# Six PSUM banks for the late tiles of an output projection, a feed-forward that starts in other banks, and a root on ScalarE

## The chip, the cores and the metric

The kernel runs on one core of a Trainium2 chip. The core has TensorE for matmuls (PE in the profile, its weight loads PEld), VectorE (DVE), ScalarE (ACT), GpSimd (POOL), a queue of DMA issues on SyncE (SP), SBUF as working memory and PSUM, eight banks of 128 partitions x 512 float32, for the results of matmuls. The metric is the device time of one execution in microseconds (us), median of several.

## The reference

One layer of a hybrid trunk in float32: 2048 tokens with 16 meta tokens ahead of them, model width 1024. What matters here:

```python
mixed = concat([lru_group, forgetting_attention, rwkv7_group]) @ w_out      # 1024 x 1024
h = h + rms_norm(mixed, norm_mix_post)
f = causal_dwconv(rms_norm(h, norm_ffn_pre) @ ffn_up, ffn_conv)             # 1024 -> 2 x 2816
gate, val = split(f)
f = (gelu(gate) * val) @ ffn_down                                           # 2816 -> 1024
h = h + rms_norm(f, norm_ffn_post)

def rms_norm(x, g):
    return x * rsqrt(mean(x * x, axis=-1) + 1e-6) * g
```

Each norm needs one reciprocal root for each token: a column of 128 values for a tile of 128 tokens.

## The kernel before, in words

The program is a line of stages: input projection beside the recurrences, attention, output projection, up projection of the feed-forward, down projection. Every matrix product is done with operands split in a high and a low part: three matmuls (L150, L151, L152) for each product of 128 rows. The up and down projections use seven products of half-size operands for eight (Strassen's scheme), whose operands are sums made on POOL and split by ACT (high, L1528) and DVE or POOL (low, L1529).

**The output projection** (`w_out_tile`, L1421) goes over 17 tiles of tokens, one of two tokens and sixteen of 128, numbered 0 to 16. For a tile it loads the mixed heads (raw, L143), splits them into `mh` (ACT, L144) and `ml` (DVE, L145), two buffers each, and computes two halves of 512 columns. A half takes 24 matmuls into one PSUM bank. Then `add_normed` (L1444) squares both halves on ACT with the sums in two columns (L1450), adds these (DVE, L1451), finds the reciprocal root with a seed from the bits and three Newton steps on 128 x 1 columns (DVE, L84 to L89, in `rstd_from`), scales the halves in their banks (L1456) and adds them to the residual (L1457), which is the last reader of the bank. The result is stored (L1440), and a second sum of squares (ACT, L96) and a second root (L84 to L89 on `rsv`) prepare the norm of the feed-forward. `mh` also takes the unused outputs of the squares.

`Banks` (L1399) hands out the banks of the halves. Up to tile 7 they come from two banks in turn (`ps_wo`); then `wide` is set, and a third bank joins (`ps_wo2`, the one that `ps_more` had during attention). Tiles 0 to 6 are mixed into attention, and tiles 7 and 8 (`HELD`) are held until attention's last step but one, so that they fill PE in its last step.

**PSUM.** In attention five banks are one pool (`ps_at`: two for maxima and sums, two for scores, one for values), `ps_more` has one and `ps_wo` two. After attention `ps_n` (two banks, for the transposes of `ffn_norm`) and `ps_f0` (three banks) take the place of the five. After the output projection `ps_f1` takes the three banks of `ps_wo` and `ps_wo2`. One unit of the up projection (342 tokens of two blocks by 128 columns of gate and value) uses three banks x, y, z; the units alternate between `ps_f0` and `ps_f1`. With `turn = 0` ahead of the loop (L1654) the first unit has `ps_f1`.

**Beside the late tiles**, from tile 8 on, the feed-forward is prepared: `ffn_norm` (L1484) loads finished tiles again, scales them (L1490) and transposes them (L1495) into the operands' quarters, POOL makes the sums of the first weights (L1601) and of the quarters (L1523), and as many operands as have memory are split: `uw0` (four weights) and `xo0` to `xo2` (three token operands). The other weights (`uw1`) and `xo3` to `xo7` lie in memory that the output projection's pool `wp` holds to its end.

**Order.** The program text gives each instruction a priority, and a planner puts the instructions of each engine in an order by simulating them; at run time each engine goes through its own list strictly in order and waits on semaphores. Pools marked `early` wait only for the tiles that lay in the same memory.

Lines that the change touches: `rstd_of` (L93), `Banks` (L1399 to L1408), `add_normed` (L1451, L1452), `turn` in `ffn_up` (L1654), the construction of `Banks` (L1996) and the line that sets `wide` (L2007). `add_normed` is also called by `Down.second` in the down projection, sixteen times.

Of the kernel before, what the change touches and what calls it, by code (L numbers as in the profile page):

```python
# [8 lines left out]
F32 = mybir.dt.float32  # L9
# [3 lines left out]
AF = mybir.ActivationFunctionType  # L13
ALU = mybir.AluOpType
# [4 lines left out]
P = 128  # L19
D = 1024  # L20
# [4 lines left out]
EPS = 1e-6  # L25
# [7 lines left out]
class Core:  # L33


    def __init__(self, tc, ctx):
        self.tc = tc
        self.nc = tc.nc
        self.ctx = ctx
        self.uid = 0  # L40
        nc = self.nc
        self.const = ctx.enter_context(tc.tile_pool(name="const", bufs=1))
        self.ident = self.const.tile([P, P], F32, name="ident")
        make_identity(nc, self.ident[:])
        self.flip = 0

    def n(self, s):
        self.uid += 1
# [41 lines left out]
    return y  # L90


def rstd_of(core, v, src, width, junk):  # L93

    ss = v[:, 4:5]
    core.nc.scalar.activation(junk, src, AF.Square, accum_out=ss)  # L96
    return rstd_from(core.nc, v, ss, width)

# [1300 lines left out]
class Banks:  # L1399


    def __init__(self, core, pools):
        self.core, self.pools, self.wide, self.turn = core, pools, False, 0

    def next(self):
        self.turn = (self.turn + 1) % 3 if self.wide else 0
        third = self.turn == 2
        return self.pools[third].tile([P, 512], F32, tag="wo", name=self.core.n("pswo"), bufs=1 if third else 2)  # L1408


def w_out_load(core, pool, w_out):
# [32 lines left out]
def add_normed(core, pool, halves, rows, gain, x, junk):  # L1444

    nc = core.nc
    v = pool.tile([P, 8], F32, tag="rs2", name=core.n("rs2"))
    s0, s1 = v[:rows, 4:5], v[:rows, 5:6]
    for c, acc in ((0, s0), (1, s1)):
        nc.scalar.activation(junk[c][:rows], halves[c][:rows], AF.Square, accum_out=acc)  # L1450
    nc.vector.tensor_tensor(s0, s0, s1, op=ALU.add)  # L1451
    r1 = rstd_from(nc, v[:rows], s0, D)  # L1452
    for c in range(2):
        cs = slice(512 * c, 512 * c + 512)
        y = halves[c][:rows]
        nc.vector.scalar_tensor_tensor(y, y, r1, gain[:rows, cs], op0=ALU.mult, op1=ALU.mult)  # L1456
        nc.vector.tensor_tensor(x[:rows, cs], x[:rows, cs], y, op=ALU.add)  # L1457
# [165 lines left out]
def ffn_up(core, raws, ring, pool, banks, w_up, cw, scr, between, tokens):  # L1623

    nc = core.nc
    tt, stt = nc.vector.tensor_tensor, nc.vector.scalar_tensor_tensor
    turn = 0
    units = [(sup, j) for sup in range(SUPERS) for j in range(NFF)]  # L1630
    ahead = UpWeights(core, raws, ring, w_up, scr, 0, 0)
    ws = [ahead.operand(i) for i in range(7)]
    xs = [tokens(0, i) for i in range(7)]

    def conv(src, u, j, n):
        y = pool.tile([P, FBLK], F32, tag="uy", name=core.n("uy"), bufs=UY)
        cc = u * NFF + j
        nc.scalar.activation(y[:, :n], src[:, 2 : n + 2], AF.Copy, scale=cw[:, 88 + cc : 89 + cc])  # L1638
        for i in (1, 0):
            stt(y[:, :n], src[:, i : n + i], cw[:, 44 * i + cc : 44 * i + cc + 1], y[:, :n], op0=ALU.mult, op1=ALU.add)  # L1640
        if u == 0:
            nc.scalar.activation(y[:, :n], y[:, :n], AF.Gelu_apprx_tanh)
        return y

    def ending(g, v, j, b0, n):
        core.pooled = nc.gpsimd.tensor_tensor(v[:, :n], g[:, :n], v[:, :n], op=ALU.mult)  # L1646
        nc.sync.dma_start(scr["ff"][P * j : P * j + P, b0 : b0 + n], v[:, :n])

    for at, (sup, j) in enumerate(units):
        b0 = [FBLK * (2 * sup + i) for i in range(2)]  # L1650
        n = [min(FBLK, SEQ - b) for b in b0]
        s = lambda tag: pool.tile([P, FN], F32, tag=tag, name=core.n(tag), bufs=1 if tag == "u2" else 2)[:]
        between(sup, j)
        more = at + 1 < len(units)  # L1654
        if more:
            ahead = UpWeights(core, raws, ring, w_up, scr, *units[at + 1][::-1])
        ws_next, bank = [], {}
        turn ^= 1
        for i, (name, (_, _, at_)) in enumerate(PRODUCTS.items()):
            w, x = ws[i], xs[i]  # L1660
            first = at_ not in bank
            if first:
                bank[at_] = banks[turn].tile([P, 512], F32, tag="up", name=core.n("psu"))[:, :FN]
            ps = bank[at_]
            for k in range(HK):
                mm3(nc, ps, w[:, 0, k], w[:, 1, k], x[:, 0, k], x[:, 1, k], first and k == 0, k == HK - 1, not first)
            if j == NFF - 1 and more:
                xs[i] = tokens(sup + 1, i)
            if more:
                ws_next.append(ahead.operand(i))  # L1670
            if name == "p1":
                ga = s("ga")
                nc.scalar.activation(ga, ps, AF.Copy)
            elif name == "p5":
                vb = s("vb")
                nc.scalar.activation(vb, ps, AF.Copy)
            elif name == "p6":
                u2 = s("u2")
                nc.scalar.activation(u2, ps, AF.Copy)
            elif name == "p3":  # L1680
                tt(ps, ps, u2, op=ALU.add)
                gb = conv(ps, 0, j, n[1])
            elif name == "p7":
                tt(vb, ps, vb, op=ALU.add)  # L1684
                vb = conv(vb, 1, j, n[1])
            elif name == "p2":
                tt(ps, ps, ga, op=ALU.add)
                ga = conv(ps, 0, j, n[0])
                ending(gb, vb, j, b0[1], n[1])
            else:  # L1690
                va = conv(ps, 1, j, n[0])
                ending(ga, va, j, b0[0], n[0])
        ws = ws_next
# [137 lines left out]
LATE = 8  # L1831
# [59 lines left out]
def hybrid_block_kernel(ctx: ExitStack, tc: tile.TileContext, args, out):  # L1891
    a = {s: v[0] if s != "meta_tokens" else v for s, v in args.items()}
    nc = tc.nc
    core = Core(tc, ctx)
# [86 lines left out]
    with ExitStack() as p3:  # L1981
# [11 lines left out]
        rs = {}  # L1993
        with p2:
            ps_wo.append(pool(p2, "ps_wo2", 1, space=PSUM, **right))
            banks = Banks(core, ps_wo)  # L1996
            g_post = spread(pool(p2, "gpost", 1, **right), a["norm_mix_post"], "g_post")
            wp = pool(p2, "wp", 2, **right)
            w = w_out_load(core, wp, a["w_out"])
# [2 lines left out]
            for i, (f, rows) in enumerate(FFN_TILES):  # L2002
                with tc.issue_after(at.steps[-2].ins) if i in HELD else nullcontext():
                    _, rs[i] = w_out_tile(
                        core, wp, banks, scr, w, x, meta, g_post, f + META - HALO, rows, rsv[:, 6 * i : 6 * i + 6]
                    )
                banks.wide = i >= LATE - 1  # L2007
                if i >= LATE and todo:
                    q, f, rows = todo.pop(0)
                    ffn_norm(core, np_, ps_n, scr, f, rows, rs[q], g_fpre, quarters[0], 0)  # L2010
                    if not todo:
                        run(ffn_sums(core, quarters[0]))
# [106 lines left out]
```

## Time and profile before

| what | value |
|---|---|
| median of three runs | 3123.35 us (3115.73 to 3134.21) |
| profiled execution | 3122.89 us |
| its span, first to last instruction | 3121.2 us |
| mean granted clock of TensorE | 0.962 |
| PE busy | 2925.9 us (94%) |
| DVE, ACT, POOL busy | 2251.1, 1452.4, 1301.9 us |
| output projection's last tiles beside the preparation | about 1632 to 1715 us |
| first matmul of the up projection | 1720.22 us |

In the profile a row of groups reads: line, engine, operation, output <- input tiles, shapes, count, busy time. A row of a timeline reads: start, duration, engine, line, operation, tiles, count, and in brackets the idle time of the engine ahead of it and what ended that. A row of waits reads: engine, tile and line that waited, engine, tile and line that it waited for, total, times, longest. A row of stretches reads: from:to, length, then busy time and count of PE, PEld, DVE, ACT and POOL (the engines with nothing to show are left out when one tile is asked for), granted clock, share and rate of the DMA engines. `psu` are banks of the up projection, `pswo` of the output projection, `psd` of the down projection, `pst` transposes, `sc`, `po` and `mx` the scores, values and maxima of attention.

### The profile page before, as it was taken

What the parts mean: (1) busy time and instruction counts of PE and PEld (TensorE: products, weight loads), DVE (VectorE), ACT (ScalarE), POOL (GpSimd) and SP (SyncE); (2) the same over time, 40 slices, a digit from 0 to 9 for tenths busy, and PEclk for the clock granted to TensorE, in tenths of its full rate; (3) what the DMA queues carried; (4) which work ended last, traced back from release to release, by engine and by line L of the source; (5) the groups of instructions that cost most, each with busy time, mean ns of one, the idle gap of its engine ahead of it and who ended that gap; (6) DMA issues with size and microseconds to landing.
All of it is one profiled execution on the core that took longest, in us unless ns stands there. A gap on an engine that the chain in (4) does not pass through costs nothing. (4 is left out here: it accounts for less than half of the span.)

```text
span 3121.2 us, 52484 instructions
## 1 busy us (share of the span) xinstructions
PE 2925.9 (94%) x18488; PEld 2492.2 (80%) x18488; DVE 2251.1 (72%) x4585; ACT 1452.4 (47%) x2716; POOL 1301.9 (42%) x1436
## 2 busy tenths in 40 slices
PE   6988999999978999999998899999999999999998
PEld 6987998999855664665576899899999999787776
DVE  6247655676688778877758898888778787547777
ACT  4135334344544444445533555566666665324332
POOL 3310001101134365446733568743533334547665
PEclk9999999999988788999999899999999999999999
DMA  6664333353353235544236555565665565535454
GB/s 205 226 204 137 101 97 100 107 140 104 97 143 81 64 84 142 130 117 107 65 107 201 162 171 158 167 193 170 166 166 166 166 188 162 174 105 167 143 161 142
DMA packets 456503, 443.72 MB, mean 142 GB/s; under 512 B 82496, under 2 KB 373514, under 8 KB 453408
## 3 DMA queue, kind: packets, MB, share of 16 engines
q1 hardware_dynamic: 455856, 439.99, 48.3%
q8 instruction: 145, 2.38, 0.3%
q14 instruction: 118, 0.97, 0.1%
q0 software_dynamic: 384, 0.39, 0.0%
HBM read 314.39 MB, written 125.87 MB: 141 GB/s over the span
## 5 line engine op out<-in xcount | busy, mean ns | idle before, releaser
L150 PE MATMUL psu<-xo,uw 128*128 128x344 f32 x1848 | 594.9, 326 | 25.2 <-DVE vb L1684 10.4
L151 PE MATMUL psu<-xo,uw 128*128 128x344 f32 x1848 | 597.1, 323 | 0.7 <-DVE xo L1529 0.7
L152 PE MATMUL psu<-xo,uw 128*128 128x344 f32 x1848 | 586.5, 322 | 0.0
L150 PE MATMUL psp<-xh,wh 128*128 128x384 f32 (+2 forms) x1152 | 382.0, 332 | 0.0
L152 PE MATMUL psp<-xh,wl 128*128 128x384 f32 (+2 forms) x1152 | 379.1, 330 | 3.0 <-DVE wl L145 3.0
L151 PE MATMUL psp<-xl,wh 128*128 128x384 f32 (+2 forms) x1152 | 378.2, 328 | 0.0
L150 PEld LDWEIGHTS psu<-xo,uw 128*128 128x128 f32 x1848 | 350.3, 190 | 31.4 <-DVE vb L1684 12.4
L1529 DVE TENSOR_TENSOR uw<-uq,uw 128x512 fp32r<-128x512 f32 x352 | 327.5, 935 | 59.5 <-ACT uw L1528 55.8
L151 PEld LDWEIGHTS psu<-xo,uw 128*128 128x128 f32 x1848 | 351.7, 190 | 1.1 <-DVE xo L1529 1.1
L152 PEld LDWEIGHTS psu<-xo,uw 128*128 128x128 f32 x1848 | 350.0, 190 | 0.0
L1528 ACT ACTIVATE uw<-uq 128x512 fp32r<-128x512 f32 x462 | 286.9, 627 | 102.8 <-PE psu L152 48.8
L640 ACT ACTIVATE p<-sc,bias 128x512 f32<-128x512 f32 (+4 forms) x352 | 197.6, 590 | 217.3 <-PE sc L636 181.8
L1640 DVE SCALAR_TENSOR_TENSOR uy<-psu,ffn_cols,uy 128x342 f32<-128x342 f32 (+1 forms) x396 | 224.0, 567 | 72.0 <-ACT uy L1638 70.9
L679 POOL TENSOR_TENSOR acc<-acc,p 128x512 f32<-128x512 f32 (+3 forms) x208 | 230.5, 1111 | 78.7 <-DVE acc L679 37.9
L1646 POOL TENSOR_TENSOR uy<-uy,uy 128x342 f32<-128x342 f32 (+1 forms) x132 | 146.3, 1109 | 224.5 <-DVE uy L1640 79.2
L152 PEld LDWEIGHTS psp<-xh,wl 128*128 128x128 f32 x1152 | 220.1, 191 | 10.3 <-issue 5.5
L150 PEld LDWEIGHTS psp<-xh,wh 128*128 128x128 f32 x1152 | 219.9, 191 | 7.1 <-issue 4.7
L151 PEld LDWEIGHTS psp<-xl,wh 128*128 128x128 f32 x1152 | 220.0, 191 | 6.4 <-issue 4.1
L1529 POOL TENSOR_TENSOR uw<-uq,uw 128x512 fp32r<-128x512 f32 x110 | 155.9, 1417 | 164.2 <-ACT uw L1528 137.8
L512 DVE TENSOR_REDUCE mc<-mx 128x1 f32<-128x400 f32 (+5 forms) x320 | 171.5, 554 | 55.3 <-PE mx L509 53.9
L1529 DVE TENSOR_TENSOR fo<-u,fo 128x896 fp32r<-128x896 f32 x88 | 104.4, 1187 | 118.6 <-ACT fo L1528 118.6
L1528 ACT ACTIVATE fo<-u 128x896 fp32r<-128x896 f32 x88 | 81.0, 922 | 230.9 <-POOL u L1756 120.9
(451 smaller groups left out, 6612.6 us busy)
## 6 DMA issues: line engine op xcount, KB each, us to landing
uq<-in_ffn_up_dram SPq DMA_DIRECT2D x220, 256.0 KB
uq<-scr_us SPq DMA_DIRECT2D x176, 256.0 KB
raw<-in_w_in_dram SPq DMA_DIRECT2D x72, 512.0 KB
scr_us<-uq SPq DMA_DIRECT2D x88, 256.0 KB
u<-scr_ff SPq DMA_DIRECT2D x88, 256.0 KB
scr_ff<-uy SPq DMA_DIRECT2D x110, 171.0 KB
q<-scr_qh SPq DMA_DIRECT2D x96, 128.0 KB
ds<-in_ffn_down_dram SPq DMA_DIRECT2D x10, 1024.0 KB
```

The lines of the kernel that those rows point to most:

```text
L150: nc.tensor.matmul(out, ah, bh, start=first, stop=False, skip_group_check=more)
L151: nc.tensor.matmul(out, ah, bl, start=False, stop=False, skip_group_check=more)
L152: nc.tensor.matmul(out, al, bh, start=False, stop=last, skip_group_check=more)
L512: self.reduced = nc.vector.tensor_reduce(mc[:rows, i, ci : ci + 1], ps[:rows, :full], axis=AX.X, op=ALU.max)
L640: last = nc.scalar.activation(p[:rows, :w], ps[:rows, :w], AF.Exp, bias=bias[:rows, j : j + 1])
L679: eng.tensor_tensor(a, ps_[0][0][:rows, c0:n] if start and i == 1 else a, p[:rows, : n - c0], op=ALU.add)
L1528: core.nc.scalar.activation(hi, src, AF.Copy)
L1529: (eng or core.nc.vector).tensor_tensor(lo, src, hi, op=ALU.subtract)
L1640: stt(y[:, :n], src[:, i : n + i], cw[:, 44 * i + cc : 44 * i + cc + 1], y[:, :n], op0=ALU.mult, op1=ALU.add)
L1646: core.pooled = nc.gpsimd.tensor_tensor(v[:, :n], g[:, :n], v[:, :n], op=ALU.mult)
```

## The change

Three things change.

1. From tile 8 on the halves go round a ring of six banks: the three of `ps_f0` first, then the two of `ps_wo`, then `ps_wo2`. Tile 8 has two of `ps_f0`, tile 9 the third and one of `ps_wo`, tile 10 the second of `ps_wo` and `ps_wo2`, and so on in threes of tiles; tile 14 has two of `ps_f0`, tile 15 the third and one of `ps_wo`, tile 16 the other and `ps_wo2`. The tag is that of the up projection's banks, so that both share the three buffers of `ps_f0`.
2. `turn` begins with 1, so that the first unit of the up projection has `ps_f0`, and the second `ps_f1`.
3. From tile 8 on (`core.root`) the reciprocal root is made in another way: the mean of one half with epsilon on DVE, a square root on ACT that takes the other half's sum scaled and the first as its bias, and a reciprocal on DVE. Where one square gave the sum of 1024 columns (L96), two squares of 512 now give two sums. The flag is not set back.

```diff
+        self.root = False
...
+def rstd_root(core, v, sums, width):
+
+    nc = core.nc
+    ms, y = v[:, 0:1], v[:, 2:3]
+    nc.vector.tensor_scalar(ms, sums[1], 1.0 / width, EPS, op0=ALU.mult, op1=ALU.add)
+    nc.scalar.activation(y, sums[0], AF.Sqrt, scale=1.0 / width, bias=ms)
+    nc.vector.reciprocal(y, y)
+    return y
+
+
 def rstd_of(core, v, src, width, junk):
 
     ss = v[:, 4:5]
+    if core.root:
+        half = width // 2
+        sums = ss, v[:, 5:6]
+        for i, acc in enumerate(sums):
+            cs = slice(half * i, half * i + half)
+            core.nc.scalar.activation(junk[:, cs], src[:, cs], AF.Square, accum_out=acc)
+        return rstd_root(core, v, sums, width)
     core.nc.scalar.activation(junk, src, AF.Square, accum_out=ss)
     return rstd_from(core.nc, v, ss, width)
...
-        self.core, self.pools, self.wide, self.turn = core, pools, False, 0
+        self.core, self.pools, self.wide, self.turn = core, pools, False, -1
 
     def next(self):
-        self.turn = (self.turn + 1) % 3 if self.wide else 0
-        third = self.turn == 2
-        return self.pools[third].tile([P, 512], F32, tag="wo", name=self.core.n("pswo"), bufs=1 if third else 2)
+        if not self.wide:
+            pool, tag, n = self.pools[-2]
+        else:
+            self.turn += 1
+            ring = [p for p in self.pools for _ in range(p[2])]
+            pool, tag, n = ring[self.turn % len(ring)]
+        return pool.tile([P, 512], F32, tag=tag, name=self.core.n("pswo"), bufs=n)
...
-    nc.vector.tensor_tensor(s0, s0, s1, op=ALU.add)
-    r1 = rstd_from(nc, v[:rows], s0, D)
+    if core.root:
+        r1 = rstd_root(core, v[:rows], (s0, s1), D)
+    else:
+        nc.vector.tensor_tensor(s0, s0, s1, op=ALU.add)
+        r1 = rstd_from(nc, v[:rows], s0, D)
...
-    turn = 0
+    turn = 1
...
-            banks = Banks(core, ps_wo)
+            banks = Banks(core, [(ps_f[0], "up", 3), (ps_wo[0], "wo", 2), (ps_wo[1], "wo", 1)])
...
-                banks.wide = i >= LATE - 1
+                banks.wide = core.root = i >= LATE - 1
```

## The prediction, on record before the result was known

> **What bounds the kernel now.** I read the page first (span and busy shares), then the stretches around the change, the waits of PE there, and the timelines of PE, ACT and DVE.
>
> ```profile
> span 3121.2 us, 52484 instructions
> PE 2925.9 (94%) x18488; PEld 2492.2 (80%) x18488; DVE 2251.1 (72%) x4585; ACT 1452.4 (47%) x2716; POOL 1301.9 (42%) x1436
> ```
>
> PE sets the time: only what leaves PE idle, or makes it slow, can be won. The change touches the end of the output projection, the seam to the feed-forward and the very end. The stretches (PE, PEld, DVE, ACT, POOL busy, granted clock, DMA) show where PE lacks work:
>
> ```profile
> 1632.00:1650.00 18.00, 13.94 (x70) 10.67 (x68) 17.25 (x33) 7.17 (x14) 5.09 (x4) 1.00 1.04 337
> 1668.00:1686.00 18.00, 13.23 (x66) 10.84 (x65) 17.40 (x30) 5.13 (x9) 11.67 (x14) 0.97 0.63 193
> 1699.00:1715.00 16.00, 16.00 (x71) 13.25 (x71) 8.75 (x34) 5.39 (x11) 0.00 (x0) 1.00 0.29 99
> ```
>
> With three banks PE is full once DVE and POOL are quiet (last row). Where the feed-forward's preparation runs beside the tiles, DVE is busy 17.25 of 18 us and PE loses a quarter. The waits of PE from 1632 to 1740 name the cause:
>
> ```profile
> PE pswo L150 <- DVE wx L1457: 9.5, 4, 4.8
> PE psu L150 <- DVE wx L1457: 4.8, 1, 4.8
> ```
>
> L1457 is the last reader of a bank. The norm's chain before it is what is slow: the same Newton root, first of tile 13 beside POOL's L1523, then of tile 16 with POOL idle:
>
> ```profile
> 1674.42 0.89 DVE L1451 TENSOR_TENSOR rs<-rs 128x1 f32<-128x1 f32 x1
> 1683.25 1.42 DVE L1456 SCALAR_TENSOR_TENSOR pswo<-pswo,rs,g_post 128x512 f32<-128x512 f32 x2
> ...
> 1716.18 0.16 DVE L1451 TENSOR_TENSOR rs<-rs 128x1 f32<-128x1 f32 x1 [3.28 <-ACT mh L1450]
> 1718.16 1.42 DVE L1456 SCALAR_TENSOR_TENSOR pswo<-pswo,rs,g_post 128x512 f32<-128x512 f32 x2
> ```
>
> 8.8 us (1674.42 to 1683.25) against 2.0 us (1716.18 to 1718.16).
>
> **Part 1: six banks, and the short root, for tiles 8 to 16.** PE's timeline at the longest wait, and at the end of the projection:
>
> ```profile
> 1679.51 1.03 PE L1495 MATMUL pst<-ident,xt 128*128 128x128 f32 x8
> 1685.31 0.80 PE L150 MATMUL pswo<-woh,mh 128*128 128x512 f32 x1 [4.77 <-DVE wx L1457]
> 1688.04 0.47 PE L150 MATMUL pswo<-woh,mh 128*128 128x512 f32 x1
> ...
> 1714.81 0.39 PE L151 MATMUL pswo<-wol,mh 128*128 128x512 f32 x1
> 1715.04 0.39 PE L152 MATMUL pswo<-woh,ml 128*128 128x512 f32 x1
> 1720.22 0.65 PE L150 MATMUL psu<-xo,uw 128*128 128x344 f32 x1 [4.79 <-DVE wx L1457]
> ```
>
> At full rate one matmul starts 0.23 us after the other (1714.81 to 1715.04). After the wait six take 2.73 us (1685.31 to 1688.04) instead of 1.38: another 1.4 us lost. I assume the same after the second longest of the four waits: 9.5 + 2.8 = 12.3 us could go. Six banks give PE three more halves, 16 us (24 matmuls each), before it needs a bank again. The root falls from ten tiny DVE instructions (nine where one square gave the sum) to two on DVE and one on ACT; all three are priced below. What stays is the operand pair mh/ml, which has two buffers and is also the junk of both squares: tile i+2 can be loaded only when tile i's whole chain is through. By rows shown here and below that is 0.8 (the last square, 0.60 + 0.19), 1.1 (root), 2.7 (1.42 for L1456, two of 0.69 for L1457), 1.6 (two squares), 1.06 (L144) and 1.1 (L145, by its 1024 elements from the xo row of Part 3): about 8.4 us, under the 11 us of PE (48 x 0.23) of the tile between, so PE keeps its pace unless DVE delays the chain by 2.5 us. I take **-10 us**; bounds -12.3 (all gone) and 0 (the pair replaces the banks as the limit).
>
> The first table load is new on ACT, and no Sqrt runs in this stage before; the nearest rows:
>
> ```profile
> L1378 ACT ACT_TABLE_LOAD  x9: 1283/1283/1283, 210.7 to 1018.7; - x9
> 1620.86 0.34 DVE L713 RECIPROCAL dcol<-dcol 16x32 f32<-16x32 f32 x1
> ```
>
> Root: the mean like L1451 (0.16 alone, 0.89 beside POOL), a 128x1 activation between the 0.19 of an accumulator's read and the 0.60 of a 128x512 square, a reciprocal of at most 0.34, and two hand-overs of about 0.2: between 0.9 and 2.2, taken as 1.1 since 128x1 is nearest to the accumulator's read. Two loads (here, and once in the down projection) are 2.6 us on an engine busy 5 to 7 of 18 us above; the first delays one chain by 1.3, within the bounds. The squares of L96 become two of 0.6 + 0.19 instead of 1.06 + 0.19: +0.3 us of ACT a tile. The Trainium skill (ScalarE: Activation LUTs, What ACT_TABLE_LOAD costs) adds a drain of about 1.38 us to each load, which would make the two 5.3 us; these rows can't show it, and the sum stands without it.
>
> **Part 2: what tile 8 no longer covers.** The ring begins with ps_f0's three banks. These are banks of attention's five, and attention uses them to its last group; before, tile 8 had a ps_wo bank and the one that the maxima had left.
>
> ```profile
> 1584.05 1.27 ACT L640 ACTIVATE p<-sc,bias 128x512 f32<-128x512 f32 x2 [1.83 <-PE sc L636]
> 1585.43 0.60 ACT L1450 ACTIVATE mh<-pswo 128x512 fp32r<-128x512 f32 x1
> 1593.11 1.06 ACT L144 ACTIVATE mh<-raw 128x1024 fp32r<-128x1024 f32 x1
> 1604.77 0.26 ACT L640 ACTIVATE p<-sc,bias 16x16 f32<-16x16 f32 x1 [2.94 <-PE sc L636]
> 1617.68 0.59 ACT L707 ACTIVATE acc<-mx 1x512 f32<-1x512 f32 x1 [1.40 <-PE mx L706]
> 1611.35 1.29 POOL L703 TENSOR_TENSOR oh<-acc,oh 128x512 fp32r<-128x512 f32 x1 [6.05 <-DVE rsv L88]
> ...
> 1585.20:1604.50 19.30, 15.98 (x66) 11.81 (x64) 3.35 (x6) 1.95 (x6) 1.00 0.40 116
> ...
> 1629.28 0.45 SPq L719 DMA_DIRECT2D scr_mix<-o  x1
> 1629.78 0.58 SPq L1912 DMA_DIRECT2D g_fpre<-in_norm_ffn_pre_dram  x1
> ```
>
> Tile 7 ends at 1585.4; from there to attention's last score 66 projection matmuls (tile 8 and part of tile 9) fill PE's gaps: 15.2 us of work. Memory that attention gives back is taken only after the last user of that pool in the planned order: g_fpre's load stands right behind attention's last store L719. For ps_f0 the last user of the pool is L707. So tile 8 stands in PE's queue behind the last L705/L706, and what is queued behind that wait is all the rest of the projection. Filler left: tile 7, and tile 9's second half (its bank is a ps_wo one), whose operands come no earlier than L144 at 1593.1. Without filler, attention goes at its own pace of exps (1.27 us for two key tiles) and ends earlier, so not all 15 us is lost: seven key tiles (4.4), the rest of the last values (3) and the sum's chain (two copies of 0.6, POOL's 1.29, its matmuls) need some 11 us from 1585.4, of which PE works 19.3 - 15.2 and about 1 more, so 5 to 6 us are idle, up to 1.4 more go in a slow restart, and tile 9's half standing in the way may cost 4 more. I take **+7 us**, bounds 0 and +15.2. One thing moves the other way: L719, and with it the preparation, comes up to 12 us earlier, so DVE's load is spread.
>
> **Part 3: the seam.** Before, 20.6 us pass from the last projection matmul to 1736, with 46 matmuls done; right behind it one takes 24.00 / 153 = 0.157 us:
>
> ```profile
> 1715.40:1736.00 20.60, 13.21 (x46) 12.24 (x47) 0.00 (x0) 0.87 (x2) 0.67 0.24 76
> 1720.00:1726.80 6.80, 6.54 (x24) 6.25 (x24) 0.00 (x0) 0.00 (x0) 0.58 0.21 82
> 1736.00:1760.00 24.00, 24.00 (x153) 24.00 (x153) 8.97 (x17) 5.60 (x12) 1.00 0.62 191
> ...
> 1720.85 1.06 ACT L96 ACTIVATE mh<-wx 128x1024 fp32r<-128x1024 f32 x1 [4.70 <-issue]
> 1721.90 1.66 ACT L1528 ACTIVATE uw<-uq 128x512 fp32r<-128x512 f32 x3
> 1723.46 5.06 ACT L1528 ACTIVATE xo<-q 128x1376 fp32r<-128x1376 f32 x4
> 1729.99 0.43 ACT L1673 ACTIVATE ga<-psu 128x344 f32<-128x344 f32 x1
> 1726.01 6.09 DVE L1529 TENSOR_TENSOR xo<-q,xo 128x1376 fp32r<-128x1376 f32 x4
> ```
>
> 20.6 - 46 x 0.157 = 13.4 us lost. The unit's first three products need xo0 to xo2 and four weights, all made long before; only their banks were missing. With turn = 1 they lie in ps_f0, which tiles 14 and 15 left two halves earlier, so 36 matmuls (5.7 us) run at once. Then PE is late for xo3: its memory is wp's, so it stands behind L96 of tile 16. With E the end of the projection: the square to E+0.8, root 1.1, L1456/L1457 2.7, two squares 1.6, three uw 1.7, two evacuations 0.9, xo 1.3, its low half 1.5, makes E+11.6. PE waits 5.9 us and starts slowly again (at the clock of 0.58 the 24 matmuls of the second row lost 6.5 - 3.8 = 2.7): 8.6 instead of 13.4, **-5 us**; bounds 0 (planned behind the old order) and -13.4. The Trainium skill (TensorE: Matmul & The Clock Gate, Part 1) states half rate after an idle window of about 3.4 us, for about as long; by it the new wait costs 1.7 instead of 2.7, and the sum would be 1 us better.
>
> **Part 4: core.root stays true.** It is never reset, so the sixteen norms of the down projection take the short root too. At the very end:
>
> ```profile
> 3110.41 0.19 ACT L1450 ACTIVATION_READ_ACCUMULATOR u<-rb 128x1 f32 x1
> 3114.89 0.75 DVE L1456 SCALAR_TENSOR_TENSOR lb<-lb,rs,g_fpost 128x512 f32<-128x512 f32 x1
> 3116.82 0.69 DVE L1457 TENSOR_TENSOR hx<-hx,rb 128x512 f32<-128x512 f32 x1
> PE psd L150 <- ACT fo L1528: 7.6, 10, 3.7
> ```
>
> The last root is ready at 3114.9, 4.3 us after its squares, because it shares DVE with the other tile's work. Two DVE instructions instead of ten for both tiles free about 2.4 us: **-2.4**, bounds -3.4 (both Newton chains of some 1.7 us gone) and +1 (hand-overs dearer). Earlier roots lie beside PE's matmuls; but ACT now waits in order for DVE's mean before Sqrt, and the operands fo queue behind it, for which PE already waits 7.6 us: 0, bounds -3 and +3.
>
> **Sum:** -10 + 7 - 5 - 2.4 = -10.4: span 3110.8. The profiled execution took 3122.89, 1.7 over its span, and the median of the runs is 3123.35, 0.5 more: **3112.5 us**.
>
> **Rivals.**
> *The pair mh/ml is the limit.* For it: DVE's 17.4 of 18 us, and the chain of tile 13 alone was 8.8 us of root. Against: nearly all of that root is removed. Part 1 gives -2 instead of -10: 3120.5.
> *The lost cover decides (slower).* One mechanism, at 1585 to 1617: tile 9's half stands in front of attention's last key tiles, all 15.2 us are lost, and tile 10, whose mh is held by tile 8, waits 4.5 more (10 us of chain with the table load less 5.5 of half a tile). It decides from 17.4 us, the sum of all the gains, or 12.4 if half of part 1 fails: +19.7 - 12.4 = +7.3, 3130. For it: 66 matmuls of filler. Against: attention's own chain shortens.
> *Little is lost.* Attention closes up at its own pace (+2), part 1 is whole (-12.3), the seam gains 7: 3122.9 - 19.7 = 3103.2.
> *The change doesn't do what it says:* the planner puts the new unit behind the tail as before, and the seam keeps its 13.4; 3117.5. I count it with the first.
>
> **Chances.** Forecast 0.42, mh/ml (and no seam) 0.20, little lost 0.27, lost cover 0.11. A measurement of this kernel tells about 0.5% (15.6 us) from no change. Faster by more needs under 3107.3: three quarters of the third case, a fifth of the forecast and a little of a plan that falls well: 0.30. Slower by more needs over 3138.5, beyond the lost cover's own time: a quarter of it, and a replanned feed-forward: 0.06. The rest, 0.64. The bounds add to 3091 and 3142; 3094 to 3131 leaves two in ten out; the forecast alone has 3102 to 3122.
>
> **What would show it.** Right: no PE wait on wx L1457 in the projection; psu matmuls start within 0.3 us of the last pswo; Newton's L88/L89 absent after 1600; one ACT_TABLE_LOAD at tile 8's Sqrt; PE idle between 1586 and 1606, tile 8 behind L706. Wrong: pswo waiting for mh L144 or ml L145 instead; tile 8 still between attention's scores; the seam waiting as long; the gain or loss lying in the 1380 us after it, which would be the plan and not these steps.

## The result and the profile after

The changed kernel takes 3106.17 us (median of 9 runs, 3098.4 to 3112.43) against 3123.35 us of the kernel before beside it: a ratio of 0.9932, 95% interval 0.9910 to 0.9955, 17 us less. The forecast was 3112.5 us, with a range of 3094 to 3131. The range holds it; "within 0.5%", to which most of the chance went, does not: it is faster by 0.68%. Of the terms of the sum the first two came out in their total, the third was wrong, the fourth too small, and a gain as large as most of them was not in the sum at all.

The page of after, span and busy shares:

```profile
span 3106.3 us, 52286 instructions
PE 2921.8 (94%) x18488; PEld 2493.4 (80%) x18488; DVE 2208.1 (71%) x4322; ACT 1463.2 (47%) x2770; POOL 1318.1 (42%) x1436
```

DVE has 263 instructions and 43 us less. Where the 14.9 us between the two profiled executions come from shows the lead of after over before at the same instruction: 1.8 us at the last projection matmul, 3.4 at the 4th unit of the feed-forward (the evacuation ga<-psu on ACT), 10.2 at the 27th, 9.4 at the 66th and last, 14.9 at the end.

The output projection first. Stretches of after, in the columns of the prediction, and under them the one of before that answers to the last:

```profile
1585.20:1604.50 19.30, 16.39 (x75) 9.91 (x74) 12.91 (x29) 8.92 (x17) 8.61 (x12) 1.00 0.39 116
...
1620.00:1632.00 12.00, 5.42 (x28) 4.27 (x27) 11.96 (x17) 7.48 (x18) 6.75 (x4) 0.64 0.88 258
1632.00:1713.40 81.40, 81.34 (x373) 67.24 (x372) 46.53 (x78) 33.92 (x81) 25.57 (x20) 0.99 0.59 194
```

```profile
1632.00:1715.30 83.30, 72.32 (x330) 57.57 (x328) 73.03 (x158) 29.36 (x54) 26.63 (x24) 0.96 0.64 211
```

Before, PE idled 11.0 us from 1632 on; after, it is full there, and DVE's 73 us have become 47. But the 12 us from 1620 on hold 5.4 us of work at a granted clock of 0.64, where before PE was full. PE's waits of after from 1560 to 1760 us: none is for wx any more (L1482, before L1457). The longest:

```profile
PE psu L168 <- ACT xo L1553: 7.4, 1, 7.4
PE pst L1520 <- ACT q L56: 3.2, 1, 3.2
PE pswo L168 <- ACT mh L162: 1.9, 1, 1.9
PE pst L1520 <- DVE rsv L98: 1.8, 1, 1.8
...
PE pst L1520 <- DVE rs L98: 1.5, 1, 1.5
```

The stall at 1620, in the timelines of ACT, DVE and PE of after:

```profile
1615.55 1.28 ACT L99 ACT_TABLE_LOAD   x1
1619.22 0.29 ACT L99 ACTIVATE rs<-rs 128x1 f32<-128x1 f32 x1 [2.38 <-DVE rs L98]
1627.97 1.04 ACT L162 ACTIVATE mh<-raw 128x1024 fp32r<-128x1024 f32 x1
...
1617.85 1.27 DVE L1515 SCALAR_TENSOR_TENSOR xt<-xt,rsv,g_fpre 2x1024 f32<-2x1024 f32 x1 [5.30 <-DMA g_fpre<-in_norm_ffn_pre_dram]
1619.05 0.13 DVE L98 TENSOR_SCALAR rs<-rs 128x1 f32<-128x1 f32 x1
...
1624.07 1.12 PE L1520 MATMUL pst<-ident,xt 128*128 128x128 f32 x4 [3.24 <-ACT q L56]
1631.26 0.78 PE L168 MATMUL pswo<-woh,mh 128*128 128x512 f32 x1
```

Tile 8's mean L98, 0.13 us of work, stands in DVE's queue behind an L1515 that waited 5.3 us for g_fpre's transfer. Tile 8's norm is late, so its mh comes free late: L162 makes tile 10's from 1627.97 to 1629.01. Tile 10 begins at 1631, and until then PE has only transposes, in the last of which it still stands until 1630.49.

The seam of after, in PE's timeline and ACT's:

```profile
1713.28 0.40 PE L170 MATMUL pswo<-woh,ml 128*128 128x512 f32 x1
1713.51 0.32 PE L170 MATMUL psu<-xo,uw 128*128 128x344 f32 x1
...
1716.53 1.04 PE L1520 MATMUL pst<-ident,xt 128*128 128x128 f32 x8
1725.01 0.65 PE L168 MATMUL psu<-xo,uw 128*128 128x344 f32 x1 [7.45 <-ACT xo L1553]
1726.77 0.65 PE L168 MATMUL psu<-xo,uw 128*128 128x344 f32 x1 [1.11 <-ACT uw L1553]
1727.22 0.49 PE L169 MATMUL psu<-xo,uw 128*128 128x344 f32 x1
...
1732.38 0.42 PE L168 MATMUL psu<-xo,uw 128*128 128x344 f32 x1
1732.64 0.32 PE L169 MATMUL psu<-xo,uw 128*128 128x344 f32 x1
...
1721.15 5.05 ACT L1553 ACTIVATE xo<-q 128x1376 fp32r<-128x1376 f32 x4
```

Five matmuls of the unit already ran from 1702.73 on, among the projection's; the others start 0.23 us after the last projection matmul, as foretold. It then stops earlier and longer than foretold: 7.45 us instead of 5.9, a second wait of 1.1, and matmuls 0.29 us apart instead of 0.16 until 1732.4.

Further on, the stretch from the 4th to the 27th unit's evacuation (boundaries are the starts of ga<-psu), before and after:

```profile
1769.79:2110.20 340.41, 322.46 (x1997) 317.86 (x1996) 292.37 (x410) 191.46 (x383) 221.36 (x160) 0.98 0.56 174
```

```profile
1766.39:2099.98 333.59, 319.21 (x1990) 314.98 (x1989) 297.53 (x409) 189.40 (x384) 224.53 (x162) 0.98 0.58 180
```

The longest of PE's waits in it, before and after:

```profile
PE psu L150 <- DVE vb L1684: 10.0, 6, 3.2
PE psu L150 <- ACT ga L1673: 6.6, 4, 2.5
```

```profile
PE psu L168 <- DVE vb L1709: 12.1, 7, 3.8
PE psu L168 <- ACT ga L1698: 0.8, 1, 0.8
```

The same 23 units take 6.8 us less, though the change edits nothing in them. And the down projection, from the first pair's first square to the last pair's, before and then after; there DVE does 144 us instead of 161, and seven pairs take 210.0 us instead of 215.8:

```profile
2891.12:3106.96 215.84, 210.59 (x895) 166.48 (x895) 160.68 (x301) 67.16 (x118) 134.90 (x162) 1.00 0.48 152
```

```profile
2884.52:3094.54 210.02, 206.79 (x893) 166.96 (x893) 144.14 (x189) 71.44 (x133) 136.44 (x161) 1.00 0.47 156
```

### The profile page after: what moved, and what is told of

Read it like the earlier page. It is cut to its first block, busy times and chain, and to the rows that moved or that the text cites. A ratio compares the mean times of both kernels' runs of the same rounds, so it can differ in the third digit from the quotient of the medians.

```text
span 3106.3 us, 52286 instructions
## 1 busy us (share of the span) xinstructions
PE 2921.8 (94%) x18488; PEld 2493.4 (80%) x18488; DVE 2208.1 (71%) x4322; ACT 1463.2 (47%) x2770; POOL 1318.1 (42%) x1436
## 4 chain that ended last, share of the span: by engine, by line
PE 61%; DVE 14%; DMA 12%; POOL 5%; issue 4%; ACT 3%; SPq 0%; POOLq 0%; DVEq 0%; ACTq 0%
PE psu L168 7%; PE psu L169 7%; PE psu L170 7%; PE psp L168 4%; PE psp L169 4%; PE psp L170 4%; PE po L676 3%; PE psd L170 2%; PE psd L168 2%; PE psd L169 2%; DVE uw L1554 2%; PE mx L527 2%; DVE uy L1665 2%; PE sc L653 2%; PE pswo L170 2%
## 5 line engine op out<-in xcount | busy, mean ns | idle before, releaser
L1554 DVE TENSOR_TENSOR uw<-uq,uw 128x512 fp32r<-128x512 f32 x352 | 333.6, 954 | 53.3 <-ACT uw L1553 49.9
L170 PEld LDWEIGHTS psp<-xh,wl 128*128 128x128 f32 x1152 | 218.9, 190 | 10.4 <-issue 5.5
L1626 POOL TENSOR_TENSOR uq<-uq,uq 128x512 f32<-128x512 f32 x88 | 137.6, 1566 | 113.0 <-DMA uq<-in_ffn_up_dram 96.4
```

The costliest lines, as they stand in the source:

```text
L170: nc.tensor.matmul(out, al, bh, start=False, stop=last, skip_group_check=more)
L1554: (eng or core.nc.vector).tensor_tensor(lo, src, hi, op=ALU.subtract)
L1626: core.nc.gpsimd.tensor_tensor(raw[:], self.raw[x][:], self.raw[y][:], op=op)
```

## The experiments

Twelve kernels were run. Their medians scatter, and so do the profiled executions, mostly ahead of 1585 us, where the change does nothing (last section). So the runs are compared by their ratio to the kernel before, measured beside them, and by stages of their profiled executions, each counted from an instruction to an instruction: tile 7's end (the second square of tile 7 on ACT) to the 4th unit, the 4th to the 27th unit, and the last unit to the end.

| kernel | ratio [95%] | tile 7 to 4th unit | 4th to 27th unit | last unit to end |
|---|---|---|---|---|
| before | 1 | 184.4 | 340.4 | 491.2 |
| after | 0.9932 [0.9910, 0.9955] | 180.1 | 333.6 | 485.7 |
| e1 ring, old root | 1.0042 [1.0021, 1.0064] | 203.2 | 333.1 | 491.6 |
| e2 root, old banks | 0.9968 [0.9950, 0.9985] | 178.3 | 342.3 | 485.4 |
| e3 ring and root, first unit in ps_f1 | 0.9971 [0.9954, 0.9988] | 181.0 | 341.1 | 487.0 |
| e4 root in the down projection only | 0.9969 [0.9949, 0.9989] | 184.9 | 342.7 | 484.7 |
| e5 no ring | 0.9932 [0.9912, 0.9953] | 175.6 | 335.1 | 488.6 |
| e6 ffn_norm a tile later | 0.9946 [0.9919, 0.9973] | 181.3 | 334.2 | 487.1 |
| e7 ring from ps_wo on | 0.9918 [0.9887, 0.9949] | 179.0 | 333.4 | 485.7 |
| e8 weights in their own pool | 0.9954 [0.9932, 0.9977] | 185.3 | 335.0 | 485.0 |
| e9 g_fpre early | 0.9953 [0.9935, 0.9972] | 179.9 | 333.6 | 483.0 |
| e10 e7 and g_fpre early | 0.9914 [0.9887, 0.9941] | 175.7 | 335.2 | 482.4 |
| e11 first unit in ps_f0 only | 0.9994 [0.9972, 1.0016] | 187.2 | 336.8 | 493.3 |
| e12 old root in the down projection | 0.9957 [0.9939, 0.9975] | 180.2 | 335.1 | 492.6 |

From the 27th unit to the last all take 519.3 to 520.6 us. In the last stage the ten executions with the short root there take 482.4 to 488.6 us, the four without 491.2 to 493.3.

**e1, the ring without the short root.**

```diff
-                banks.wide = core.root = i >= LATE - 1
+                banks.wide = i >= LATE - 1
```

> Six banks and the feed-forward's first unit in ps_f0, but core.root stays False everywhere: all roots are the Newton chains of before. Theory 'plan' (most of the gain is the order that the new first bank gives the feed-forward's DVE and ACT; profiled, before minus after is 1.8 us at the projection's end, 9 us at the 22nd unit and 9.4 at the last): the 7 us between the 4th and the 27th unit are here too, the 5 us of the down projection are not; the projection is slower than after, since DVE keeps the ten-step roots: 3114 us. Theory 'path' (my prediction: banks and root win in the projection and at the seam, nothing changes after): no gain beyond the seam, 3118 to 3123 us, and with the slow root PE waits for mh or ml instead of for the banks.

Slower than before by 0.4%, and by 19 us in the projection, worse than either theory had. PE's waits there:

```profile
PE pswo L168 <- ACT mh L162: 14.2, 4, 7.0
```

No wait for wx, but four for mh: with slow roots the six banks only move the wait to the pair mh/ml, and tile 8 behind attention's end is paid on top. The stretch from the 4th to the 27th unit is as short as in after.

**e2, the short root without the ring** (three banks, first unit in ps_f1, as before; the count in `Banks` begins as before too).

```diff
-            banks = Banks(core, [(ps_f[0], "up", 3), (ps_wo[0], "wo", 2), (ps_wo[1], "wo", 1)])
+            banks = Banks(core, [(ps_wo[0], "wo", 2), (ps_wo[1], "wo", 1)])
...
-    turn = 1
+    turn = 0
```

> Three banks and the feed-forward in ps_f1 as before, the short root from tile 8 on and in the down projection. 'Plan': the feed-forward's order is that of before, so nothing is won between the 4th and the 27th unit; the projection wins 8 to 11 us (tile 8 keeps its place between attention's scores, and the waits for wx shrink from 14.3 us to under 4), the down projection 5: 3123.4 - 10 - 5 = 3108 us, as fast as the whole change. 'Path': the bank wait remains in part; 3123.4 - 5 - 2.4 = 3116 us.

Faster by 0.32%, between the two numbers. Up to the 4th unit it gains 6.1 us on before, more than the whole change (4.2), and the down projection gains 5.8; the 23 units gain nothing. Its waits for wx are 8.9 us in the projection, and 3.5 more at the first psu: 12.4 us of the 14.3 of before, where "plan" expected under 4 to be left. So the projection won less.

```profile
PE pswo L168 <- DVE wx L1482: 8.9, 5, 5.6
```

**e3, the whole change but the first unit in ps_f1.**

```diff
-    turn = 1
+    turn = 0
```

> The whole change, except that the feed-forward begins in ps_f1 as before. 'Plan': the projection's 1.8 us and the down projection's 5 stay, the 7 us between the 4th and the 27th unit are lost, and the seam's 1.6 us too: 3106.2 + 8.6 = 3115 us. 'Path': only the seam's 5 us are lost: 3111 us. If the 7 us were chance of the one profiled execution: 3106 to 3108 us.

Slower than after by 0.4% (the intervals 0.9910 to 0.9955 and 0.9954 to 0.9988 barely touch). The stretch from the 4th to the 27th unit is 7.5 us longer, as "plan" had it; the seam, from the last projection matmul to the 4th unit, takes 52.4 us against 53.1 of after. So the turn does nothing for the seam that one could see.

**e4, the short root in the down projection only.**

```diff
+        core.root = True
         ps_f.append(pool(p3, "ps_f1", 3, space=PSUM, **early))
```

(the rest as before.)

> The kernel before, with the short root in the down projection alone; everything ahead of it is planned as before. By my part 4: 3123.4 - 2.4 = 3121 us, the gain at the last root alone. By the profile of after (its lead grows from 9.4 us at the last unit to 14.9 at the end): 3123.4 - 5.5 = 3118 us, growing over all eight pairs of tiles.

Faster by 0.31%, 6.5 us in the last stage: more than twice my part 4. Seven pairs take 210.1 us, as in after, and the two numbers of before with the same plan, 184.9 and 342.7, tell how far one execution strays from another: 0.5 and 2.3 us. By its ratio e4 is as fast as e2 (0.9969 and 0.9968), which has the short root in the projection as well. The intervals leave room for the 6.1 us that e2 gains there, but only the stages show them.

**e5, the whole change without the ring.**

```diff
-            banks = Banks(core, [(ps_f[0], "up", 3), (ps_wo[0], "wo", 2), (ps_wo[1], "wo", 1)])
+            banks = Banks(core, [(ps_wo[0], "wo", 2), (ps_wo[1], "wo", 1)])
```

> The whole change without the ring: three banks as before (two of ps_wo, one of ps_wo2), but the short root and the feed-forward's first unit in ps_f0. Theory 'root and order' (the runs so far: the short root alone takes 126.0 us from tile 7's end to the last projection matmul, root and ring 127.0 and 128.6; the order of the feed-forward that comes with the earlier first unit gains 7 to 9 us): as fast as the whole change or a little faster, 3103 to 3108 us on the scale where the kernel before takes 3123; tile 8 stands between attention's scores again. Theory 'banks' (the six banks are what keeps PE full from 1632 to 1713 us): the waits for wx come back, 9 to 12 us, and it takes 3113 to 3116 us.

As fast as the whole change, ratio 0.9932 for both: "root and order". The waits for wx come back (4.1 us), but ps_f0 is free all the time, and PE does 24 matmuls of the first unit from 1673 us on, while it would wait. Tile 7 to the 4th unit is 4.5 us shorter than with the ring.

**e6, the first call of ffn_norm a tile later.**

```diff
-                if i >= LATE and todo:
+                for _ in range(0 if i <= LATE or not todo else 2 if i == LATE + 1 else 1):
```

> The whole change, with the first call of ffn_norm put off by one tile (none behind tile 8, two behind tile 9, of which one has 2 rows). Theory 'stall' (the PE time lost from 1620 to 1632 us comes from DVE standing at L1515 for 5.3 us, for g_fpre's transfer, ahead of tile 8's mean L98): that wait no longer stands ahead of tile 8's chain, 6.6 us of idle PE and about 1 us of slow restart go, 8 us less than the whole change: 3098 us on the scale where before takes 3123. Rival (tile 10 waits for mh anyway, because tile 8 lies behind attention's end and its chain is long with the table load): under 2 us. Second rival: the preparation ends later and the seam gets longer by what is won.

No gain (0.9946), and no test either: the order of the program did not move with the call, and the wait stands where it was.

```profile
1617.08 1.27 DVE L1515 SCALAR_TENSOR_TENSOR xt<-xt,rsv,g_fpre 2x1024 f32<-2x1024 f32 x1 [5.34 <-DMA g_fpre<-in_norm_ffn_pre_dram]
1618.28 0.13 DVE L98 TENSOR_SCALAR rs<-rs 128x1 f32<-128x1 f32 x1
```

Here the planned order did not follow the order of the calls.

**e7, six banks from ps_wo on.**

```diff
-            ring = [p for p in self.pools for _ in range(p[2])]
-            pool, tag, n = ring[self.turn % len(ring)]
+            pool, tag, n = self.pools[(0, 1, 0, 2, 2, 2)[self.turn % 6]]
...
-    turn = 1
+    turn = 0
```

(pools in the order ps_wo, ps_wo2, ps_f0.)

> Six banks in another order: tile 8 starts in ps_wo and ps_wo2 as before, ps_f0's banks come fourth to sixth, so that the last three halves lie in them and the feed-forward starts in ps_f1. Theory 'lost cover' (my part 2: tile 8 between attention's scores is worth what PE idled from 1585 to 1604 and from 1620 to 1632 us, 2.9 + 6.6 + about 1.4 of slow restart): from tile 7's end to the last projection matmul 127.0 - 10 = 117 us, and 3096 us on the scale of 3123. Rival 'pair' (mh and ml have two buffers; with slow roots and six banks PE waited 14.2 us for mh): PE waits for mh or ml instead, 124 us or more, and 3104 to 3107 us.

From tile 7's end to the last projection matmul it takes 125.0 us, not 117: 2 of the 10 us that the lost cover should be worth. The waits for mh and ml are small too (1.6 and 0.7), so "pair" isn't it either; the lost time is spread (transposes 2.4 us, attention's mx 4.4). And with tile 8 between attention's exps ACT loads tables two times more, at 1601.9 and 1605.2 us (so in e2, e5 and e10; in after there is one load, behind attention). The ratio 0.9918 lies below that of after, within its interval.

**e8, the weights of the output projection in a pool of their own.**

```diff
-            w = w_out_load(core, wp, a["w_out"])
+            w = w_out_load(core, wp, pool(p2, "wpk", 1, **right), a["w_out"])
```

(w_out_load takes woh and wol from it.)

> The whole change, with w_out's split weights woh and wol in a pool of their own, so that the memory of xo3 to xo6 and of uw1 is free once the last projection matmul is planned, and not only behind tile 16's whole norm. Theory 'seam' (PE waits 7.4 us for xo3, because ACT and DVE can make it only after tile 16's norm): the wait shrinks to about 3 us, 4 us less than the whole change. Theory 'hidden' (the first units of the feed-forward are held by the splitting of their weights and tokens on ACT, DVE and POOL, so that time won at the seam is lost again by the 4th unit: both turns of the first bank take 52.3 to 54.8 us from the last projection matmul to the 4th unit's first evacuation): the wait shrinks, the 4th unit's evacuation comes no earlier by more than 1.5 us, same time as the whole change.

The wait for xo shrinks to 2.2 us, as "seam" had it, but the new order puts twelve matmuls of the second unit ahead, and PE stands 8.2 us in that:

```profile
1732.95 0.42 PE L168 MATMUL psu<-xo,uw 128*128 128x344 f32 x1 [2.17 <-ACT xo L1553]
1735.12 0.42 PE L169 MATMUL psu<-xo,uw 128*128 128x344 f32 x1 [1.74 <-DVE xo L1554]
1746.26 0.62 PE L168 MATMUL psu<-xo,uw 128*128 128x344 f32 x1 [8.23 <-ACT mh L112]
```

The first evacuation comes 24.3 us after the last projection matmul instead of 13.3, 11 us late; at the 4th unit 3.8 us of that are left (56.9 against 53.1). For time lost, "hidden" holds for two thirds; that time won would be lost again in the same way was not shown.

**e9, g_fpre loaded ahead of attention.**

```diff
+        pg = ExitStack()
+        g_fpre = spread(pool(pg, "gf", 1, **right), a["norm_ffn_pre"], "g_fpre")
         p2 = ExitStack()
...
-        g_fpre = spread(pool(p3, "gf", 1, **early), a["norm_ffn_pre"], "g_fpre")
```

> The whole change, with g_fpre in memory of its own that is loaded before attention, so that no instruction waits for its transfer (putting off the call of ffn_norm by a tile had left the planned order and the 5.3 us wait as they were). Theory 'stall': DVE no longer stands at L1515 ahead of tile 8's mean L98; PE's loss between 1620 and 1632 us (6.6 us idle and about 1 of slow restart) goes, from tile 7's end to the last projection matmul 128 - 8 = 120 us, and 3098 us on the scale where before takes 3123. Rival: tile 8 lies behind attention's end and its chain holds mh for tile 10 anyway, so that PE waits for mh: 126 to 128 us as now, 3106 us.

The transfer is out of the way, the stall is not: DVE now stands at the same line for the tile's own load, and tile 8's mean comes at 1624 instead of 1619.

```profile
1620.90 1.27 DVE L1515 SCALAR_TENSOR_TENSOR xt<-xt,rsv,g_fpre 2x1024 f32<-2x1024 f32 x1 [2.45 <-DMA xt<-scr_h]
1623.19 1.28 DVE L1515 SCALAR_TENSOR_TENSOR xt<-xt,rsv,g_fpre 128x1024 f32<-128x1024 f32 x1 [1.02 <-DMA xt<-scr_h]
1624.39 0.15 DVE L98 TENSOR_SCALAR rs<-rs 128x1 f32<-128x1 f32 x1
```

The projection takes 125.8 us, 1 to 3 less than in after, e3, e6 and e12 (127.0 to 128.6), and the ratio is 0.9953. The rival was nearer: what holds tile 10 is tile 8's late chain, and g_fpre was only the first of several things ahead of it in DVE's queue.

**e10, the ring of e7, g_fpre early, first unit in ps_f0.** The edits of e7 and e9 with turn = 1.

> The ring that starts with ps_wo and ps_wo2 (tile 8 between attention's scores), g_fpre loaded early, the feed-forward's first unit in ps_f0. If lost cover and the wait for g_fpre are the two costs in the projection, it loses neither: 119 to 122 us from tile 7's end to the last projection matmul (125.0 with this ring and the late g_fpre), the feed-forward's order of the whole change, 3096 to 3099 us on the scale of 3123. If the pair mh and ml sets the pace: 125 us, 3103 us.

121.3 us in the projection, as expected, and 175.7 to the 4th unit. It has the lowest ratio of all, 0.9914 [0.9887, 0.9941]. It beats the kernel before; that it beats after (0.9910 to 0.9955) can't be told from these runs.

**e11, nothing but the first unit in ps_f0.**

```diff
-    turn = 0
+    turn = 1
```

(the kernel before.)

> The kernel before, with nothing but the feed-forward's first unit in ps_f0 instead of ps_f1: three banks, the Newton roots everywhere. Theory 'order' (the seam itself gains 0 to 2 us, but the planned order of DVE and ACT in the next 40 units changes, and that gains 7 us): 333 to 335 us from the 4th to the 27th unit's first evacuation instead of 340 to 343, the rest as before: 3123.4 - 7 = 3116 us. My part 3 (the seam gains 5 us, nothing after it): 3118 us, gained between the last projection matmul and the 4th unit. Rival (the order pays only together with the short root): 3121 to 3123 us.

No difference that can be told: 0.9994 [0.9972, 1.0016], between 9 us faster and 5 slower. The 23 units take 336.8 us, 3.6 to 5.9 less than in the four executions of the old order, but up to the 4th unit it needs 2 to 3 us more than before and e4. PE's waits for wx stay, 10.4 us in the projection. So my part 3 is out, since the stage up to the 4th unit is where its 5 us should have been won. Of the 7 us of "order" some are there; whether they stay in the total, this run leaves open.

**e12, the whole change with the old root in the down projection.**

```diff
+        core.root = False
         ps_f.append(pool(p3, "ps_f1", 3, space=PSUM, **early))
```

> The whole change, with core.root set back to False after the output projection, so that the down projection keeps the Newton roots; the planned order is that of the whole change up to there. If the down projection's gain is the short root's (485 us from the last unit's first evacuation to the end with it, 491.2 and 491.6 without): 491 us there, 127 to 129 us from tile 7's end to the last projection matmul, 333 to 335 us from the 4th to the 27th unit, and 5 us more than the whole change: 3111 us on the scale where before takes 3123. By my part 4 (2.4 us, at the last root alone): 488 us there and 3108.5 us.

The last stage takes 492.6 us, 6.9 more than after, and the two stages ahead repeat those of after to 0.1 and 1.5 us. Together with e4 this settles the down projection.

## Why the prediction was right or wrong

**Part 1 and part 2, -10 + 7 = -3.** Measured from tile 7's end to the last projection matmul: 129.6 and 131.2 us with the plan of before, 127.0, 127.0, 127.6 and 128.6 with that of after; -2.8. Both terms are there with nearly their size: PE idled 11.0 us from 1632 on and idles no more, and 2.9 + 6.6 us of idle time and a slow start are new ahead of it.

Two steps of the working failed all the same. The gain was given to "six banks, and the short root"; the root makes it. With old banks it gains 6.1 us up to the 4th unit (e2), and with old banks and the turn 11.7 (e11 to e5); with the ring and old roots 19 are lost (e1). The ring does take the waits for wx away (none in after, 12.4 us in e2), but what it adds ahead costs more: beside the short root it is 2.8 us slower up to the 4th unit (e2 to e3), and 4.5 (e5 to after). Each of these is a difference between two single executions. The pair mh/ml, the first rival, was dismissed with "nearly all of that root is removed"; that is right for after and explains e1.

The loss was put at 1586 to 1606, where only 2.9 us are lost. Tile 8 did stand behind L706 (now L724), but attention went on beside tile 7 and tile 9, and the price fell due when tile 10 waited for tile 8's mh, the chain that the prediction had only in its slower rival. What it did not have is the instruction of another job, L1515, ahead of the mean in DVE's queue. That the +7 came out nearly right is therefore luck in part: most of the loss lies at another place and has another cause.

**The root's price.** Last tile, after: the mean 1714.43, the reciprocal 1714.95, L1481 at 1715.15, so 0.7 us where 1.1 were taken. Each of the two loads of a table takes 1.28 us, and its neighbours show no more:

```profile
1714.43 0.15 DVE L98 TENSOR_SCALAR rs<-rs 128x1 f32<-128x1 f32 x1 [2.11 <-ACT mh L1472]
1714.95 0.16 DVE L100 RECIPROCAL rs<-rs 128x1 f32<-128x1 f32 x1 [0.36 <-ACT rs L99]
1715.15 1.42 DVE L1481 SCALAR_TENSOR_TENSOR pswo<-pswo,rs,g_post 128x512 f32<-128x512 f32 x2
...
2887.27 0.19 ACT L1472 ACTIVATION_READ_ACCUMULATOR u<-lb 128x1 f32 x1
2887.47 1.28 ACT L99 ACT_TABLE_LOAD   x1
2888.77 0.29 ACT L99 ACTIVATE rs<-rs 128x1 f32<-128x1 f32 x1
```

The next activation starts 0.02 us after the load's end. The drain of 1.38 us that the Trainium skill (ScalarE: Activation LUTs, What ACT_TABLE_LOAD costs) adds does not show here.

**Part 3, -5.** Measured -1.6 up to the 4th unit, and e3 has as much without the turn (52.4 against 54.7 us of before), so the turn gave nothing. Wrong was "36 matmuls run at once". In the order that the program gives PE, after the first two products (24 matmuls) and eight transposes comes one matmul of the sixth and two of the second unit, and then the third product, whose operands lie ready (transposes left out):

```
 12  psu_17771 <- xo_17742    first product
 12  psu_17789 <- xo_17745    second product
  1  psu_17876 <- xo_17757    sixth product
  2  psu_17930 <- xo_17742    second unit, first product
 12  psu_17771 <- xo_17748    third product
```

PE takes them in order, so it waited for the sixth product's xo. That came 11.7 us after the end of the projection (1725.01 - 1713.28); "E+11.6" was worked out, but for another operand, xo3 with its low half; in the trace its high half is done at 1722.48 and its low half at 1726.94, E+13.7. So the two numbers meet by luck. The chain was there, but the queue in front of it was not looked at, though the order of before had the same form. The slow start was right: from 1726.8 to 1732.4, 18 gaps of 0.287 instead of 0.157 us lose 2.3, and with the first (0.45) and the last (0.26) it is 2.7, as foretold. What was mis-sized is the wait, 7.45 + 1.1 us against 5.9, and the work ahead of it, 24 matmuls against 36. The slow spacing lasted 5.6 us, and the granted clock was 0.50 from 1722.3 to 1732.6. The Trainium skill (TensorE: Matmul & The Clock Gate, Part 1) gives about 3.4 us of work to such a start, counted by a window that runs freely; here it took longer.

**The missing term: -6.8 us in 23 units.** "What would show it wrong" named it (a gain "in the 1380 us after"), the sum did not have it. With the first unit's first bank free, its first matmuls come earlier, and DVE's and ACT's instructions of the first two thirds of the feed-forward fall into another order, though the edits change no instruction there. The order of before is also that of e2, e3 and e4 there (340.4 to 342.7 us), that of after, but for a few places near its ends, is in e1, e5 to e7 and e9 to e12, and in e8 from the 8th unit or so on (333.1 to 336.8). The two groups don't overlap. In the runs with the order of before the first unit begins 3.9 to 6.3 us after the last projection matmul, in the others 0.2 us after it or sooner. It needs no turn = 1: in e7 the unit begins in ps_f1, while the ring's last halves lie in ps_f0, and the order is that of after. How the planner comes from the one thing to the other was not looked at. In the order of before PE waited 6.6 us for ga, in that of after 0.8; an instance, in before's timelines of ACT and PE:

```profile
1985.00 0.55 ACT L1638 ACTIVATE uy<-psu,ffn_cols 128x342 f32<-128x342 f32 x1 [1.57 <-POOL uy L1646]
1985.44 0.45 ACT L1673 ACTIVATE ga<-psu 128x344 f32<-128x344 f32 x1
...
1985.94 0.42 PE L150 MATMUL psu<-xo,uw 128*128 128x344 f32 x1 [2.15 <-ACT ga L1673]
```

ga stands behind an activation that waits for POOL, and PE behind ga. But the waits in sum differ by 4 us and not by 7, and which exchange of places matters was not isolated; that stays open. So does why e11 gains only 3.6 to 5.9 us there.

**Part 4, -2.4 and 0 for the middle.** The end is as foretold: from the last down matmul (3107.52 before, 3095.10 after) to the end of the span it was 13.7 us and is 11.2, -2.5, in every run with the short root. "Earlier roots lie beside PE's matmuls: 0, bounds -3 and +3" was wrong. Seven pairs take 214.6 to 217.1 us in the four executions with Newton roots and 209.6 to 211.1 in the ten without, 0.8 us a pair: DVE is at 161 of 216 us there, it makes fo's lower halves too, and PE's wait for them (fo L1529, 1.4 us in four) is gone in after, and in e2, e4 and e5; in e11 it is there (1.1), and in e12 (2.4). With the waits go slow starts: in these pairs 29 matmuls started 0.26 to 0.6 us behind the one before, and now 8; longer gaps were 11 and are 6. The dear hand-over from DVE's mean to ACT, which was feared, did not come: PE waits as long for ACT's fo as before (3.2 against 3.1 us). PE's waits in the seven pairs, before and after:

```profile
PE psd L150 <- ACT fo L1528: 3.1, 7, 0.7
PE psd L152 <- DVE fo L1529: 1.4, 4, 0.5
```

```profile
PE psd L168 <- ACT fo L1553: 3.2, 6, 1.0
```

**Sum.** Foretold -10 + 7 - 5 - 2.4 = -10.4; in the two profiles -2.6 - 1.6 - 6.8 + 0.9 - 5.5 (projection, seam, 4th to 27th unit, 27th to last, down projection) = -15.6, with 0.8 lost ahead of tile 7's end -14.8, and -14.9 by the spans. The forecast span was 4.5 us above the profiled one: the seam's term was 3.4 too large, the last one 3.1 too small, and the missing one made the rest. That it was not 9.9 us is luck: the seam's error and smaller ones cancel more than half of the missing 6.8 and the 3.1. (The prediction names 1.7 and 0.5 us between the span and the median and adds only the first; with both it is 3113.0.) The slower rival fell at its number (no end at +7), but its mechanism, tile 8's chain holding tile 10, is what made the loss that there was.

## What to carry to other kernels

Where buffers are waited for, look at the chain that frees them before adding buffers: with the shorter chain the kernel was as fast without the new buffers as with them (0.9932), and the buffers with the old chain moved the wait to the next pair and cost 19 us. Before counting what runs "at once" when a wait goes, read the in-order queue behind it: an instruction of a later job can stand ahead, on DVE as on PE. And where a planner orders the program, a change at one place can move the time of a stretch that it does not touch by as much as it wins itself; stages counted from instruction to instruction, in several kernels, tell the two apart.

## What the runs showed of the hardware

The profiled executions differ by up to 23 us ahead of tile 7's end (1579.9 to 1602.6 us), with the same work there. Most of that lies from 900 to 1210 us, where the granted clock is lowest and differs from one execution to the next. Of e7, whose tile 7 ended at 1580.9:

```profile
900.00:1210.00 310.00, 277.40 (x2356) 181.12 (x2355) 253.80 (x760) 140.82 (x300) 150.40 (x233) 0.86 0.38 90
```

and of e11, where it ended at 1602.6:

```profile
900.00:1210.00 310.00, 277.11 (x2290) 184.41 (x2289) 240.64 (x717) 127.75 (x278) 135.52 (x221) 0.78 0.34 80
```

At a clock of 0.78 PE is as busy and has done 66 matmuls less. Of the 21.7 us between these two, 15.4 arise between attention's first exp (893.2 and 894.3 us) and its 101st (1149.5 and 1166.0). In a single execution the 23 us are 0.7% of this kernel, as much as the whole change; what sets the clock there, no run shows.

In the clock records of all fourteen traces the granted clock is either full or one half, so that 0.78 is a mean over stretches of both. But for the last of each execution, the stretches at one half last whole multiples of 3.41 us: three of them, 10.2 us, at the seam of after, beginning 4.7 us after PE had fallen idle.
